# Four dense blocks instead of two in the head of a hybrid block, two of them before the norm is known

## The chip, the cores and the metric

The kernel runs on one core of a Trainium2 chip. The metric is the device time of one execution in microseconds; the median of three runs of the kernel before is 904.12 us. TensorE is PE in the profile, its weight loads PEld, VectorE is DVE, ScalarE is ACT, GpSimd is POOL, and SyncE, which issues most DMAs here, is SP.

## The reference, cut to what matters

One layer, 512 positions, width 1024. Only the first projection and what hangs on it matter here:

```
h    = rmsnorm(x) * g
P    = h @ w_in            # columns: attention q,k,v | RWKV r,k,v, decay, iclr, gate lora | branch gates
A    = stick_breaking_attention(q, k, v)              # 8 heads of 64
xs   = token_shift(P_rwkv, mu)                        # p + (previous p - p) * mu
w    = decay_base + tanh(w_lo) @ decay_up;  iclr = sigmoid(iclr_base + a_lo @ iclr_up)
y    = rwkv7_recurrence(r, decay, k, v, -kk, kk*iclr) # 8 heads of 64, chunks of 64 positions
x    = x + (sigmoid(gate_0) * (A @ W0) + sigmoid(gate_1) * (B @ W1)) @ w_out
x    = x + W_down(silu(c_g) * c_v),  [c_g, c_v] = causal conv3(rmsnorm(x) @ W_up)
```

The norm multiplies every position of h by one number, rs. A projection of x*g can therefore be multiplied by rs afterwards, before the token shift.

## The kernel before, in words

Activations lie with channels on partitions (8 tiles of 128) and the 512 positions on the free axis. Every fp32 operand of a dense product is split in a high part (fp32r) and the rest; a product of two is three matmuls: high by high, high by rest, rest by high. A **dense block** gives 128 columns of a projection: 8 tiles of the contraction by 3 is 24 matmuls of 128x128 by 128x512. Its weight comes by one DMA (load_w, line 102), ScalarE casts the high part (line 104), ScalarE writes minus the high part (line 117) and a DMA issued by GpSimd adds the raw weight to it (line 118). There are two raw and two high buffers and four of half a rest.

The **head** (lines 198 to 310) loads x (line 211), the weights of two blocks (line 206) and the small matrices; squares x on ScalarE, sums the squares over partitions by a matmul with a constant matrix (line 228), and makes rs with a logarithm and an exponential. Then, tile by tile, it makes xn = x g rs on VectorE (line 238), the high part on ScalarE (line 239) and the rest on VectorE or GpSimd (line 240), with six matmuls to each tile (lines 242 to 245): the lora block (pl0) and k of RWKV's first pair of heads (pk0). lora's result becomes wal and, by a tanh, wl1 and wl2; the two small matrices become lup (lines 269 to 271).

What follows is written by **a planner** (interleave). Six streams, one of dense blocks (dense_stream), one that runs the attention of four pairs of heads in turn (att_stream), and four of RWKV (rw_stream, one to a pair of heads), yield costs, delays (LAT) and events; the planner keeps a clock of its own and writes the instructions in the order that this clock gives. PE and SP execute in exactly that order; the other engines' order is chosen by the framework. A dense block is taken when no other stream is ready, or when a deficit has grown; RWKV's blocks are taken when the event prep of the pair before is near, then those of the attention, else a branch gate (evac_gate, line 785), of which 13 are written here.

A pair of RWKV goes through: two lora products (line 393), the norm of k (lines 153 and 154 by blk2), preparation (lines 438 to 468) with the same pair of lines at its end, four groups of transposes and products (lines 484 and 489), two stores and loads through DRAM, a **solve** of 31 steps on VectorE (lines 520 and 522), again a turn through DRAM to U1 and TT, the products that start from U1 (line 543), eight chunks one after another (lines 590 to 616), a norm, and the output gate (line 640). LAT says at what moment of the planner's clock something is due: k0=42000 holds all of pair 0 after lora back, and the second block of the stream as well; solve is about 50000.

When all streams have ended, what is left (three gates, w_branch, w_out, the feed-forward part) follows and is not touched by the change.

Of the kernel before, what the change touches and what calls it, by code (L numbers as in the profile page):

```python
# [8 lines left out]
F32 = mybir.dt.float32  # L9
F32R = mybir.dt.float32r  # L10
# [42 lines left out]
def hybrid_block(ctx: ExitStack, tc: tile.TileContext, xT, w_in, vecs, decay_up, iclr_up, out_gate_up,  # L53
# [24 lines left out]
    def f(ap):  # L78
        return ap.bitcast(F32)
# [17 lines left out]


    def load_w(src, nk):
# [4 lines left out]
        A.copy(hi[:, 0:nk], raw[:, 0:nk])  # L104
        w = (hi, [], raw)
        for _ in range(1 if nk <= 4 else 2):
            load_w2(w, nk)
        return w
# [87 lines left out]
    with tc.tile_pool(name="p0", bufs=1) as p0, \  # L196
# [10 lines left out]

        w0, w1 = wtiles(), wtiles()
        A.dma_start(vec, vecs[:, 0:NVEC1])
# [10 lines left out]
        V.tensor_copy(none_, tmpc)  # L220
        pl0, pn, pk0, rs = bank(psr, "pr"), bank(psr, "pr"), bank(), bank(psz, "pz")

        for k in range(0, KT, 2):
            sq = [p0.tile([P, T], F32, tag=f"sq{j}", name=f"sq{j}", bufs=2) for j in range(2)]
            for j in range(2):
                act(sq[j], xt[:, k + j], AF.Square)
            V.tensor_tensor(sq[0], sq[0], sq[1], op=ALU.add)
            PE.matmul(pn, f(none_), sq[0], start=(k == 0), stop=(k == KT - 2))
        act(rs, pn, AF.Ln, scale=-1.0 / D, bias=eps_n)
        act(rs, rs, AF.Exp, scale=-0.5)  # L230
        for w in (w0, w1):
            for h in range(2):
                A.copy(w[0][:, 4 * h : 4 * h + 4], w[2][:, 4 * h : 4 * h + 4])
                load_w2(w)

        for k in range(KT):
            xn = p0.tile([P, T], F32, tag="xn", name="xn", bufs=3)
            V.scalar_tensor_tensor(xn, xt[:, k], vcol("ag", k), rs, op0=ALU.mult, op1=ALU.mult)
            A.copy(hhi[:, k], xn)
            (V if k % 2 else G).tensor_tensor(hlo[:, k], xn, f(hhi[:, k]), op=ALU.subtract)  # L240
            for ps, w in (pl0, w0), (pk0, w1):
                PE.matmul(ps, w[0][:, k], hhi[:, k], start=(k == 0), stop=False)
                PE.matmul(ps, w[1][k // 4][:, k % 4], hhi[:, k], start=False, stop=False)
            for ps, w in (pl0, w0), (pk0, w1):
                PE.matmul(ps, w[0][:, k], hlo[:, k], start=False, stop=(k == KT - 1))
        state["dma"] = True
# [7 lines left out]
        V.tensor_scalar(qg8, vcol("qg"), 0.125, None, op0=ALU.mult)  # L254
        wfirst = load_w(w_in[:, RW0 : RW0 + P], KT)
        wal = p0.tile([P, T], F32, name="wal")
        shift_evac(wal, pl0, 12)
# [8 lines left out]
        for j in range(2):  # L266
            hr, ho = slice(64 * j, 64 * j + 64), slice(64 - 64 * j, 128 - 64 * j)
            lt = p0.tile([P, BW], F32R, tag="lt", name="lt")
            A.copy(lt, lraw[j])
            V.tensor_tensor(lup[j][ho], lraw[j][ho], f(lt[ho]), op=ALU.subtract)  # L270
            A.copy(lup[j][hr], lraw[j][hr])

# [74 lines left out]

    def evac_rw(p, which, ps):
        RD[p][which] = rwp.tile([P, T], F32, tag="x" + which, name="x" + which)
        shift_evac(RD[p][which], ps, 4 * "rkv".index(which) + p)  # L350
# [448 lines left out]
    def dense_stream():  # L799
        rwq, atq = [], []  # L800
        for p in range(4):
            for i, w in (1, "k"), (0, "r"), (2, "v"):
                if (p, w) != (0, "k"):
                    rwq.append((RW0 + i * BW + p * P, evac_rw, (p, w), w + str(p), (f"prep{p - 1}",)))
# [16 lines left out]

        evac_rw(0, "k", pk0)
        yield ("set", "k0", LAT["k0"])
        yield ("set", "bank-1", LAT["k0"])
        i, cur = 0, pick()
        nxt = wfirst
        while cur:
# [14 lines left out]
            else:  # L842
# [13 lines left out]
    FULL, SHORT = 0.65, 450  # L856
    LAT = dict(evac=5520, ahead=11059, k0=42000, gl0=1, gl1=2, att0=(1332, 762, 1125, 1575),
               att1=(810, 810, 810, 688), gn=(659, 3062, 2114, 3270), hop=(1073, 1254, 767, 762),
               lup=(8543, 2168, 5055, 862), pl=(671, 2115, 609, 2223), prep=(9000, 9000, 9000, 9000),
               pu=(1860, 2060, 1022, 1951), qk=(1409, 1644, 4330, 575), rw0=(792, 1679, 2305, 1342),  # L860
               solve=(46500, 49755, 50000, 50000), sq=(2447, 1872, 3786, 557), sq_a=(1958, 1741, 1565, 328),
# [206 lines left out]
```

## Time and profile before

| | |
|---|---|
| median of 3 runs | 904.12 us (903.95 to 909.15) |
| profiled execution | 908.44 us, of it 906.6 us span |
| PE busy | 864.9 us, 95% of the span, 4722 matmuls |
| PEld, DVE, ACT, POOL busy | 74%, 60%, 56%, 14% |
| chain that ended last | PE 80%, ACT 6%, DVE 5%, DMA 5%, issue 2% |

Busy time is a union of spans, and a matmul's span is longer than its distance to the next, so a PE that is shown as full need not be at its fastest. The distance from one matmul's start to the next one's is the better measure, and the moments at which the stages begin are better still.

### The profile page before, as it was taken

To read this page: it belongs to the slowest core of one execution; us is meant where nothing else is said; L and a number is where in the kernel's file an instruction comes from. 1 tells how busy PE (TensorE), PEld (TensorE's weight loads), DVE (VectorE), ACT (ScalarE), POOL (GpSimd) and SP (SyncE) were. 2 spreads that over 40 slices of the span, in tenths; PEclk is the share of its full clock that TensorE was granted. 3 is DMA by queue.
4 is the path that set the end of the run, shared out by engine and by line. 5 is a ranking of instruction groups with operands and counts; after the bars stand their busy time and mean duration, and the time that the engine had idled before them with its cause. 6 is when DMAs were issued, how large, how long until landed. Compare 5 with 4: busy or idle time off the path is not lost.

```text
span 906.6 us, 12925 instructions
## 1 busy us (share of the span) xinstructions
PE 864.9 (95%) x4722; PEld 668.4 (74%) x4722; DVE 544.6 (60%) x1104; ACT 508.0 (56%) x900; POOL 129.9 (14%) x200
## 2 busy tenths in 40 slices
PE   4988988999999999899999999999999999999998
PEld 2666756676767677667888888888888888888886
DVE  5466796685785484246565556777777777522222
ACT  6787877866875784688654445444444444311120
POOL 2323333224322332223000000000000000000000
PEclk8999999998999999999999999999999999999999
DMA  8276556556548445852654543333333333243431
GB/s 230 53 147 132 112 128 116 126 121 126 120 84 184 106 94 111 165 127 73 228 190 135 149 122 92 98 93 93 94 99 106 97 94 94 87 128 99 124 102 41
DMA packets 175135, 106.94 MB, mean 118 GB/s; under 512 B 29568, under 2 KB 156672, under 8 KB 175072
## 3 DMA queue, kind: packets, MB, share of 16 engines
q1 hardware_dynamic: 161392, 81.61, 32.1%
q0 software_dynamic: 10656, 19.40, 12.7%
q10 hardware_dynamic: 3024, 5.11, 1.6%
q8 instruction: 37, 0.61, 0.3%
q14 instruction: 26, 0.21, 0.1%
HBM read 78.31 MB, written 8.39 MB: 96 GB/s over the span
## 4 chain that ended last, share of the span: by engine, by line
PE 80%; ACT 6%; DVE 5%; DMA 5%; issue 2%; SPq 1%; POOL 1%; POOLq 0%; ACTq 0%
PE pf L130 17%; PE pf L131 17%; PE pf L132 17%; PE pd L847 15%; DMA wraw<-in_w_in 2%; DMA wlo<-wraw 1%; DVE tm L520 1%; SPq L529 1%; ACT whi L104 1%; PE pz L730 1%; PE pr L603 1%; PE pr L489 1%; PE pr L590 1%; ACT wlo L117 1%; ACT t L69 1%
## 5 line engine op out<-in xcount | busy, mean ns | idle before, releaser
L104 ACT CAST whi<-wraw 128x1024 fp32r<-128x1024 f32 (+1 forms) x132 | 130.0, 985 | 192.6 <-PE pf L131 143.6
L120 DVE TENSOR_TENSOR wlo<-wraw,whi 128x512 fp32r<-128x512 f32 (+1 forms) x178 | 114.5, 680 | 81.6 <-ACT whi L104 75.7
L130 PE MATMUL pf<-h2h,whi 128*128 128x512 f32 x352 | 137.3, 390 | 0.0
L131 PE MATMUL pf<-h2l,whi 128*128 128x512 f32 x352 | 136.9, 389 | 0.0
L132 PE MATMUL pf<-h2h,wlo 128*128 128x512 f32 x352 | 136.9, 389 | 0.0
L847 PE MATMUL pd<-hhi,whi 128*128 128x512 f32 x296 | 122.8, 415 | 6.5 <-ACT gs L785 2.8
L847 PE MATMUL pd<-hlo,whi 128*128 128x512 f32 x296 | 121.8, 411 | 0.0
L118 POOL DMA_DIRECT2D wlo<-wraw x74 | 65.1, 912 | 191.6 <-ACT wlo L117 111.8
L847 PE MATMUL pd<-hhi,wlo 128*128 128x512 f32 x296 | 86.0, 409 | 2.8 <-DMA wlo<-wraw 2.7
L131 PEld LDWEIGHTS pf<-h2l,whi 128*128 128x128 f32 x352 | 66.1, 188 | 13.9 <-issue 0.2
L132 PEld LDWEIGHTS pf<-h2h,wlo 128*128 128x128 f32 x352 | 66.1, 188 | 13.8
L130 PEld LDWEIGHTS pf<-h2h,whi 128*128 128x128 f32 x352 | 66.1, 188 | 13.8 <-issue 0.2
L847 PEld LDWEIGHTS pd<-hhi,whi 128*128 128x128 f32 x296 | 56.8, 192 | 20.5 <-ACT gs L785 3.3
L132 PE MATMUL pf<-dh,wlo 128*128 128x512 f32 x176 | 69.3, 394 | 0.0
L130 PE MATMUL pf<-dh,whi 128*128 128x512 f32 x176 | 69.3, 394 | 0.0
L131 PE MATMUL pf<-dl,whi 128*128 128x512 f32 x176 | 69.3, 394 | 0.0
L847 PEld LDWEIGHTS pd<-hhi,wlo 128*128 128x128 f32 x296 | 53.6, 190 | 17.4 <-DMA wlo<-wraw 5.9
L847 PEld LDWEIGHTS pd<-hlo,whi 128*128 128x128 f32 x296 | 56.8, 192 | 11.7 <-issue 0.5
L1007 DVE TENSOR_TENSOR u<-pf,rs 128x512 f32<-128x512 f32 x44 | 30.3, 688 | 38.7 <-PE pf L132 38.6
L124 ACT CAST dh<-cv 128x512 fp32r<-128x512 f32 x22 | 13.7, 621 | 62.0 <-DVE cv L1016 62.0
L117 ACT ACTIVATE wlo<-whi 128x512 fp32r<-128x512 f32 x74 | 45.5, 630 | 1.9 <-ACT QA L598 0.7
L130 PEld LDWEIGHTS pf<-dh,whi 128*128 128x128 f32 x176 | 32.9, 187 | 8.3
(303 smaller groups left out, 1609.6 us busy)
## 6 DMA issues: line engine op xcount, KB each, us to landing
wraw<-in_w_up SPq DMA_DIRECT2D x44, 512.0 KB, 3.7
wraw<-in_w_in SPq DMA_DIRECT2D x42, 512.0 KB, 3.9
wlo<-wraw POOLq DMA_DIRECT2D x74, 256.0 KB, 3.9
wraw<-in_w_down SPq DMA_DIRECT2D x16, 512.0 KB, 4.0
wraw<-in_w_branch SPq DMA_DIRECT2D x16, 256.0 KB, 2.9
wraw<-in_w_out SPq DMA_DIRECT2D x8, 512.0 KB, 4.0
gd<-gs ACTq DMA_DIRECT2D x13, 256.0 KB, 3.3
g<-gd SPq DMA_DIRECT2D x13, 256.0 KB, 2.9
```

Source lines behind the costliest of these rows:

```text
L69: ins = A.activation(o, i, func, **kw)
L104: A.copy(hi[:, 0:nk], raw[:, 0:nk])
L117: A.mul(lo[:, 0:n], f(hi[:, k0 : k0 + n]), -1.0)
L118: G.dma_start(lo[:, 0:n], raw[:, k0 : k0 + n], accum_op=ALU.add)
L120: V.tensor_tensor(lo[:, 0:n], raw[:, k0 : k0 + n], f(hi[:, k0 : k0 + n]), op=ALU.subtract)
L124: A.copy(hi, src)
L130: PE.matmul(ps, hi, ah, start=first, stop=False)
L131: PE.matmul(ps, hi, al, start=False, stop=False)
L132: PE.matmul(ps, lo, ah, start=False, stop=last)
L489: PE.matmul(pp[h][:, j * P : (j + 1) * P], BK[hr, ch].rearrange("p s t -> p (s t)"), ARV[hr, ch, 0 : 2 + h : 1 + h], start=True, stop=True)
L847: PE.matmul(ps, w_, a, start=(n == 0), stop=(n == len(todo) - 1))
L1007: V.tensor_tensor(u, ps, rs2, op=ALU.mult)
```

## The change

In the head, four blocks are computed. x and the weights are loaded in turns, in the order x0, half of w0, x1, half of w0, x2 and x3, half of w1, x4 and x5, half of w1, x6 and x7, w2, w3. As each tile of x lands, x g is split in high and rest and multiplied by lora's weight (w0) and, three tiles behind, by k's (w1); the rest-by-high matmuls of both come after. Then rs is made, and the same buffers are filled again with the normalised x, tile by tile, for r (w2) and v (w3) of pair 0. lora's result and k's are multiplied by rs afterwards (ul, and u in evac_rw), from a copy rss. The stream loses the blocks r0 and v0 and starts with q of the attention's first pair. k0, r0 and v0 are due 4000 after the stream's start (before: k0 at 42000), and rw0 goes from 792 to 2500. Some instructions of ScalarE are tied behind the last high part of the normalised x: the table load for tanh, the casts for lup, the high part of the first weight of the stream.

```
-        for k0, k1 in ((0, 1), (1, 2), (2, 4), (4, 6), (6, 7), (7, 8)):
-            nc.sync.dma_start(xt[:, k0:k1], xv[:, k0:k1])
-        wdma(w0, LR0, 0, 8)
-        wdma(w1, RW0 + BW, 0, 8)
+        nc.sync.dma_start(xt[:, 0:1], xv[:, 0:1])
+        wdma(w0, LR0, 0, 4)
...
+        wdma(w2, RW0, 0, 8)
+        wdma(w3, RW0 + 2 * BW, 0, 8)
...
+        def first(w, ps, k, part):
+            PE.matmul(ps, w[0][:, k], h_acts[k][part], start=(k + part == 0), stop=False)
+        def second(w, ps, k):
+            lo = w[1][k // 4][:, k % 4] if isinstance(w[1], list) else w[1][:, k]
+            PE.matmul(ps, lo, hhi[:, k], start=False, stop=(k == KT - 1))
+        LAG = 3
+        for k in range(KT):
+            if k % 4 == 0:
+                A.copy(w0[0][:, k : k + 4], w0[2][:, k : k + 4])
+            act(hhi[:, k], xt[:, k], AF.Identity, scale=vcol("ag", k))
+            V.scalar_tensor_tensor(hlo[:, k], xt[:, k], vcol("ag", k), f(hhi[:, k]), op0=ALU.mult, op1=ALU.subtract)
+            for part in range(2):
+                first(w0, pl0, k, part)
+            sq[k] = p0.tile([P, T], F32, name=f"sq{k}")
+            sql = act(sq[k], xt[:, k], AF.Square)
+            if k % 4:
+                V.tensor_tensor(sq[k & 4], sq[k & 4], sq[k], op=ALU.add)
+            if k % 4 == 3:
+                A.copy(w1[0][:, k - 3 : k + 1], w1[2][:, k - 3 : k + 1])
+            if k >= LAG:
+                for part in range(2):
+                    first(w1, pk0, k - LAG, part)
+            if k % 4 == 3:
+                PE.matmul(pn, f(none_), sq[k & 4], start=(k == 3), stop=(k == 7))
...
+        first_parts(w2, sql)
+        second_parts(w2, sql)
         act(rs, pn, AF.Ln, scale=-1.0 / D, bias=eps_n)
         act(rs, rs, AF.Exp, scale=-0.5)
...
-            A.copy(hhi[:, k], xn)
+            state["last"] = A.copy(hhi[:, k], xn)
             (V if k % 2 else G).tensor_tensor(hlo[:, k], xn, f(hhi[:, k]), op=ALU.subtract)
+            if k == 1:
+                first_parts(w3, state["last"])
+            if k == 3:
+                second_parts(w3, state["last"])
+            for part in range(2):
+                first(w2, pr0, k, part)
+            if k >= 2:
+                for part in range(2):
+                    first(w3, pv0, k - 2, part)
+            if k >= LAG:
+                second(w2, pr0, k - LAG)
...
+        after(A.copy(rss, rs), state["last"])
...
+        V.tensor_tensor(ul, pl0, rss, op=ALU.mult)
+        shift_evac(wal, ul, 12)
         load_set(SET_SG, (AF.Sigmoid, AF.Tanh))
+        after(state["load"], state["last"])
...
-                if (p, w) != (0, "k"):
+                if p > 0:
...
-        evac_rw(0, "k", pk0)
-        yield ("set", "k0", LAT["k0"])
-        yield ("set", "bank-1", LAT["k0"])
+        evac_rw(0, "k", pk0, by=rss)
+        evac_rw(0, "r", pr0)
+        evac_rw(0, "v", pv0)
+        for w in "krv":
+            yield ("set", w + "0", LAT["k0"])
+        yield ("set", "bank-1", LAT["evac"])
```

first_parts casts the high part of a weight in two halves on ScalarE; second_parts writes minus the high part on ScalarE and adds the raw weight by a DMA of GpSimd, as load_w2 does.

## Rows read from the trace of the kernel before

**Rows 1.** Stretches of the span: busy time and instructions of each engine, PEclk, DMA share, GB/s.

```profile
5.00:19.00 14.00, 7.42 (x8) 2.13 (x8) 7.28 (x14) 8.77 (x15) 0.00 (x0) 0.96 0.84 231
33.00:61.00 28.00, 24.58 (x95) 16.97 (x96) 11.09 (x16) 26.29 (x44) 10.46 (x15) 1.00 0.63 122
86.00:130.00 44.00, 40.61 (x191) 29.99 (x190) 36.91 (x98) 38.65 (x85) 18.36 (x26) 1.00 0.54 119
150.00:300.00 150.00, 145.60 (x1208) 107.12 (x1209) 102.34 (x286) 107.87 (x225) 42.13 (x67) 0.97 0.60 127
550.00:600.00 50.00, 50.00 (x222) 41.42 (x221) 37.39 (x56) 22.82 (x29) 0.00 (x0) 1.00 0.32 95
```

**Rows 2.** Timeline of the head: start, length, engine, line, operation, tiles.

```profile
3.62 1.32 ACT L69 ACTIVATE sq<-xt 128x512 f32<-128x512 f32 x2 [1.53 <-DMA xt<-in_xT]
...
11.57 0.63 ACT L69 ACTIVATE sq<-xt 128x512 f32<-128x512 f32 x1 [0.54 <-PE pr L228]
...
17.07 1.28 ACT L63 ACT_TABLE_LOAD   x1
...
18.36 0.62 ACT L239 CAST hhi<-xn 128x512 fp32r<-128x512 f32 x1
...
19.04 0.80 PE L242 MATMUL pr<-hhi,whi 128*128 128x512 f32 x1 [4.23 <-ACT hhi L239]
...
27.40 0.62 ACT L239 CAST hhi<-xn 128x512 fp32r<-128x512 f32 x1 [0.88 <-DVE xn L238]
...
32.23 0.39 PE L245 MATMUL pr<-hlo,whi 128*128 128x512 f32 x1
...
32.46 0.39 PE L245 MATMUL pd<-hlo,whi 128*128 128x512 f32 x1
...
32.66 1.04 ACT L104 CAST whi<-wraw 128x1024 fp32r<-128x1024 f32 x1 [4.63 <-PE pr L245]
...
33.75 0.50 PE L847 MATMUL pd<-hhi,whi 128*128 128x512 f32 x1 [0.91 <-ACT whi L104]
```

**Rows 3.** Stretches of 1 us in the head, columns as in rows 1.

```profile
18.00:19.00 1.00, 0.00 (x0) 0.00 (x0) 1.00 (x3) 0.99 (x3) 0.00 (x0) 0.50 0.00 0
...
25.00:26.00 1.00, 1.00 (x6) 0.83 (x5) 0.87 (x2) 0.93 (x3) 0.71 (x1) 1.00 0.00 0
```

**Rows 4.** ACT's groups, 33 to 87 us: count | busy us, mean ns | idle before.

```profile
L117 ACT ACTIVATE wlo<-whi 128x512 fp32r<-128x512 f32 x14 | 8.2, 619 | 0.0
L104 ACT CAST whi<-wraw 128x1024 fp32r<-128x1024 f32 x7 | 7.3, 1043 | 9.5 <-DMA wraw<-in_w_in 4.9 <-PE pr L245 4.6
```

**Rows 5.** Last products ahead of the solve, pairs 0 to 3: ns min/median/max, first and last start.

```profile
L489 PE MATMUL pr<-ARV,BK x32: 272/272/524, 71.2 to 85.7; 64*128 64x128 f32 x32
...
L489 PE MATMUL pr<-ARV,BK x32: 272/272/325, 138.6 to 155.4; 64*128 64x128 f32 x32
...
L489 PE MATMUL pr<-ARV,BK x32: 272/272/362, 206.1 to 217.2; 64*128 64x128 f32 x32
...
L489 PE MATMUL pr<-ARV,BK x32: 272/272/325, 292.1 to 306.0; 64*128 64x128 f32 x32
```

**Rows 6.** First products behind the solve, pairs 0 to 3, columns as in rows 5.

```profile
L543 PE MATMUL pr<-U,QA x32: 184/191/212, 150.0 to 150.5; 32*32 32x32 f32 x32
...
L543 PE MATMUL pr<-U,QA x32: 184/236/258, 219.0 to 220.5; 32*32 32x32 f32 x32
...
L543 PE MATMUL pr<-U,QA x32: 191/191/212, 286.7 to 287.2; 32*32 32x32 f32 x32
...
L543 PE MATMUL pr<-U,QA x32: 191/191/212, 375.1 to 375.6; 32*32 32x32 f32 x32
```

**Rows 7.** What PE waited for, 30 to 432 us: us in total, times, longest.

```profile
PE pr L543 <- DMA U<-st: 4.1, 3, 2.5
```

**Rows 8.** End of the streams: the last gates' copies and pair 3's output gate.

```profile
L785 ACT COPY gs<-pd x4: 587/588/623, 395.1 to 433.1; 128x512 f32<-128x512 f32 x4
...
L640 PE MATMUL pr<-gl,ogu x1: 399/399/399, 422.5 to 422.5; 96*128 96x512 f32 x1
```

More of the change, by code (lines that the diff above doesn't have):

```diff
@@ L96, in vcol, with after @@
         return vec[:, o : o + w] if o < NVEC1 else state["vec2"][:, o - NVEC1 : o - NVEC1 + w]
+    def after(ins, other):
+        tc.add_manual_dep(ins.ins, other.ins.name, _ORDER, reason="order")
     def load_w(src, nk):
@@ L103, in load_w @@
         hi = wpool.tile([P, KT, P], F32R, tag="whi", name="whi")
-        A.copy(hi[:, 0:nk], raw[:, 0:nk])
+        after(A.copy(hi[:, 0:nk], raw[:, 0:nk]), state["last"])
         w = (hi, [], raw)
@@ L220, in hybrid_block @@
         V.tensor_copy(none_, tmpc)
[L221 to L228, printed above, removed]
+        pl0, pn, pk0, pr0 = bank(psr, "pr"), bank(psr, "pr"), bank(), bank()
@@ new lines, in hybrid_block, with first_parts, second_parts @@
+        for w in (w0, w1):
+            load_w2(w)
+            load_w2(w)
+        for k in range(KT - LAG, KT):
+            for part in range(2):
+                first(w1, pk0, k, part)
+        for k in range(KT):
+            second(w0, pl0, k)
+            second(w1, pk0, k)
+        def first_parts(w, other):
+            for k in (0, 4):
+                after(A.copy(w[0][:, k : k + 4], w[2][:, k : k + 4]), other)
+        def second_parts(w, other):
+            for k in (0, 4):
+                after(A.mul(w[1][:, k : k + 4], f(w[0][:, k : k + 4]), -1.0), other)
+                G.dma_start(w[1][:, k : k + 4], w[2][:, k : k + 4], accum_op=ALU.add)
@@ L229, in hybrid_block @@
+        first_parts(w2, sql)
+        second_parts(w2, sql)
         act(rs, pn, AF.Ln, scale=-1.0 / D, bias=eps_n)
         act(rs, rs, AF.Exp, scale=-0.5)
[L231 to L234, printed above, removed]
+        rss = keep.tile([P, T], F32, tag="rs", name="rss")
         for k in range(KT):
@@ L268, in hybrid_block @@
             lt = p0.tile([P, BW], F32R, tag="lt", name="lt")
-            A.copy(lt, lraw[j])
+            after(A.copy(lt, lraw[j]), state["last"])
             V.tensor_tensor(lup[j][ho], lraw[j][ho], f(lt[ho]), op=ALU.subtract)
-            A.copy(lup[j][hr], lraw[j][hr])
+            after(A.copy(lup[j][hr], lraw[j][hr]), state["last"])
         ident = cpool.tile([P, P], F32, name="ident")
@@ L346, in hybrid_block, with evac_rw @@
     AD = [dict() for _ in range(4)]
-    def evac_rw(p, which, ps):
+    def evac_rw(p, which, ps, by=None):
+        if by is not None:
+            u = rwp.tile([P, T], F32, tag="u", name="u")
+            V.tensor_tensor(u, ps, by, op=ALU.mult)
+            ps = u
         RD[p][which] = rwp.tile([P, T], F32, tag="x" + which, name="x" + which)
```

33 lines of the change are left out of this document (24 added, 9 removed).

## The prediction

> **What bounds the kernel now.** I read the stretches first. Behind the streams PE is full and no other engine is near it (550 to 600 us in [rows 1]): nothing there is touched, so the question is only at what moment the streams end. They end at 433.1 us, with the last gate's copy [rows 8]. In the head PE is busy for 7.42 of 14 us while it waits for x and for rs, and ACT for 8.77 [rows 1]. From 33 to 61 us the picture turns: ACT is busy for 26.29 of 28 us, PE for 24.58 by spans that flatter it. From 86 to 130 us ACT is at 38.65 and DVE at 36.91 of 44. From 150 to 300 us no engine but PE is above three quarters, and PE's instructions are in an order written ahead, so small waits add up in it [rows 1].
>
> Then I marked the stages of the four RWKV pairs by two lines: the last product ahead of the solve (S: 85.7, 155.4, 217.2, 306.0) [rows 5] and the first one behind it (B: 150.0, 219.0, 286.7, 375.1) [rows 6]. From S to B a pair takes 64.3, 63.6, 69.5, 69.1 us, and PE waited in three of four cases for U1 itself, 4.1 us in all [rows 7]. So the solve and its two turns through DRAM are nearly as late as PE's order: neither alone sets the end.
>
> **The change, part by part.**
>
> *PE in the head.* Between matmuls 0.23 us pass (32.23 to 32.46, [rows 2]), so a block is 24 x 0.227 = 5.45 us. Before, two blocks end at 32.85, the stream starts at 33.75 [rows 2], and r0 and v0 cost it 10.9 us. After: the last of x landed for the square at 11.57 [rows 2]; now 1 MB of weights goes in turns with it, at the head's 231 GB/s [rows 1] at most 4.5 us; bounds 11.6 and 16, taken 13.7, as three of the four halves lie ahead of where x would otherwise be at the end. On ACT each tile now has a high part beside the square, 16 x 0.62 and four half casts, 12.4 us by full lengths, from the first landing at 3.6 [rows 2]: 16, so ACT and the last landing agree on about 16.3 for the last square. From the last square's start to the first normalised high part 6.8 us passed (11.57 to 18.36), 1.28 of it the table load that is now tied behind [rows 2]: 5.5 us. w2's four casts can slip in between at 0.62 each, 0 to 2.5. So the first normalised tile is cast at about 21.9 + 0.6 (bounds 20.5 and 24); the eight took 9.0 us (18.36 to 27.40, [rows 2]) and take as long again, since VectorE's and GpSimd's work on a tile is unchanged: 31.2. Behind the last tile about 20 matmuls are left, 4.5 us: PE ends the head at **35.8** (33.5 to 39). It is two blocks ahead of before at 32.85 + 0.9 + 10.9 = 44.7: a credit of 8.9 us.
>
> *ACT.* Two weights of the stream move into the head, 2 x (1.04 + 2 x 0.62) = 4.6 us [rows 4]. But the table load (1.28), four casts for lup (0.62 each) and the copy rss (0.6), of which the first five lay in ACT's idle time in the head, are now behind the last tile [rows 2]: 4.4 us. ACT's stage begins at 31.2 instead of 32.66. While ACT is full, which is so at least to 61 us, 1.5 us is all that can be cashed of the credit. The extra multiplications by rs are two of VectorE, 0.7 us each, which has 17 us idle from 33 to 61 [rows 1]; on the way of tanh and lup the first one is exposed, with rss and the table load about 3 us, and lup's product (third of the stream's groups) is where PE meets them: 0 to 4 us, inside S0 below.
>
> *The order that is planned.* Following the planner's rule with the new numbers (for the order alone): ahead of S of pair 0 stand q, k, v of attention, a gate, the two gate-lora blocks, another gate, and five of the eight attention jobs of pair 0. Before, it is r0, v0, q, k, v and most of a gate, and no job. Between S and B stand 7, 6, 6, 7 blocks, as before. Between B of pair 0 and S of pair 1: the solve's loads are now planned just behind the last group. Between B of pair 1 and S of pair 2: two more blocks and the four groups, where before S came first. Behind B of pair 3: two blocks instead of five, and no attention job where before there were all eight.
>
> *Queues.* On SP w2, w3 and the half-weights go ahead of the small matrices; nobody needs these before 31 us. On POOL two DMA adds of w2 and two of w3 stand among the four splits; w3's are wanted last of all. These cost nothing as long as a pair of adds ends in the 8 us that they have; if not, the head's end moves with them, inside its bound.
>
> **The sum**, against the profiled execution (908.44 us, 4.3 above the median; the difference is carried over to the median):
> - S of pair 0, before 85.7. At before's pace from a stream start of 35.8: 52 us, 1.4 blocks more (7.6) and five jobs at about a microsecond of PE (5): 100.4. Lower bound: the 3.4 us of PE idle of 33 to 61 and as many again are gone, 93.5. Upper bound: ACT sets it; all eight jobs lie in 86 to 130 with 38.65 us of ACT [rows 1], so five add at most 24: 85.7 - 1.5 + 24 = 108. Taken 100: **+14.3**. It is a loss that buys work done ahead.
> - S to B, four times: the same cover, and VectorE has half of pair 0's attention behind it in the first solve. Bounds -12 and 0; taken **-4**.
> - B0 to S1: 5.4 us become -1: **-6.4**.
> - B1 to S2: -1.8 become +18 (four groups 11.1 us with what lies between them [rows 5], one more block 5.45, a little): **+19.8**.
> - B2 to S3: 19.3 less a group and half a block: **-5.5**.
> - B3 to the end: 58.0 us (375.1 to 433.1); three blocks fewer, 16.4, and eight jobs fewer, some 8, but pair 3's chain alone is then what runs; taken 36 (bounds 33 and 47): **-22**.
>
> Together -3.8 us: 904.6 by the profiled execution, **900.3** on the median. The 8.9 us of credit is mostly spent on waiting for ACT and on a last pair with nothing beside it.
>
> **The rivals.**
> - *The credit is kept.* If PE rather than ACT sets S of pair 0 (93.5, so 6.5 less), and the solves come 8 us shorter in all because VectorE and ACT meet less work at once, 14 us more are gained, with half of it about 893 and with all of it 886; 890 as its centre. For it: no engine but PE is over three quarters from 150 us on [rows 1]. Against: ACT's 26.29 of 28.
> - *Slower: the last pair's chain.* From B of pair 3 to its output gate 46.9 us passed (375.1 to 422.0, from the four matmuls that end at 422.5 [rows 8]). If the eight chunks take that long by their own latency, whether or not blocks lie between them, the tail is 47 instead of 36: +11, so 911; with S of pair 0 at 104 it is 915. It decides from a tail of 40 us on. For it: each chunk waits for the one before. Against: five blocks and eight jobs of PE lie in that stretch.
> - *The first pass doesn't bring its end forward* (the change doesn't do what it says): x lands behind the weights, or PE's clock stays low. After its idle time PE had a granted clock of 0.50 from 18 us on, which is the 1.2 GHz level, and was back at 1.00 by 25 us, after about 5 us of matmuls [rows 3]. At 0.45 us instead of 0.227 the 22 matmuls between the sums and the normalised tiles cost 4.9 us more, and part of that is hidden under ACT's eight casts: head's end 39.3, time 900 to 904, say 903. The Trainium skill says (TensorE: Matmul & The Clock Gate, HAM oscillation — how this bites in real kernels) that bursts of matmuls with waits for DMA between them are set back to the low clock each time, which speaks against matmuls that follow the landing of x. The rows here show one such fall and no series of them; by that rule the head would end at 39.3 and this rival holds, otherwise 35.8.
>
> **How the numbers follow.** Chances: forecast 0.42, credit kept 0.30, last pair's chain 0.18, no earlier end 0.10. A measurement of this kernel tells about 1% from no change, 9 us: faster means below 895.1, slower above 913.2. Of the credit's 0.30 about 0.26 lies below 895, and of the forecast's 0.42 about 0.08: faster 0.34. Of the chain's 0.18 half lies over 913, and of the forecast (S at its upper bound with nothing given back) 0.07: slower 0.16. The rest, 0.50, is no change. The range goes from the credit's far end, 886, to the chain's 912.
>
> **What would show it.** PE's last head matmul at 33.5 to 39 us; normalised casts from 22 us; PE's clock in the first pass; S of pair 0 at 94 to 108 us with ACT full ahead of it; S to B of 60 to 69 us four times; S of pair 2 about 18 us behind B of pair 1; a tail of 33 to 40 us behind B of pair 3, with PE idle in it; everything behind the streams as long as before, 473 us. The prediction is wrong if S of pair 0 comes before 90 us, if the solves become clearly shorter than 60 us, or if PE has a long wait that is not in this list.

## The result: 1.4% slower, and the profile after

The changed kernel takes 917.96 us (median of 4 runs, 915.99 to 920.82) against 904.04 for the kernel before (903.61 to 909.15): a ratio of 1.0143, interval 1.0097 to 1.0189. Forecast were 900.3 us and a range up to 912. The profiled execution took 915.99 us, span 914.3. That is 7.5 us more than the profiled execution of before, 6 us less than the medians differ by: the profile of before is one of its longer runs, that of after the shortest of its four (and of the runs below, 2 and 3 lie further off in the execution that was profiled, 925.37 us against a median of 918.84 and 937.63 against 920.78, so the columns of run 3 are left empty). The rows below answer to 7.5 us.

One sentence of the description ahead of the prediction is to be corrected. TensorE takes exactly the written order only in the head block. In the streams the planner's order is what is written, but the framework may still move one of TensorE's instructions past another: both lora products (L469) stand ahead of all of q's matmuls in the machine, though the planner writes q first.

The head first, as a timeline of the kernel after (start, length, engine, line, operation; in brackets the idle time and what ended it). It answers to [rows 2].

```profile
31.15 0.62 ACT L294 CAST hhi<-xn 128x512 fp32r<-128x512 f32 x1 [2.99 <-DVE xn L293]
...
36.25 1.07 PE L245 MATMUL pr<-hhi,w3l 128*128 128x512 f32 x4
39.83 0.50 PE L469 MATMUL pr<-wl,lup 128*128 128x512 f32 x1 [2.51 <-ACT wl L336]
...
42.38 0.68 DVE L342 TENSOR_TENSOR lup<-lraw,lt 64x512 fp32r<-64x512 f32 x1 [2.45 <-ACT lt L341]
42.99 0.68 DVE L423 TENSOR_TENSOR u<-pd,rss 128x512 f32<-128x512 f32 x1
...
43.21 0.77 PE L469 MATMUL pr<-wl,lup 128*128 128x512 f32 x1 [2.45 <-DVE lup L342]
...
44.63 0.80 PE L927 MATMUL pd<-hhi,whi 128*128 128x512 f32 x1
...
52.01 0.39 PE L927 MATMUL pd<-hhi,whi 128*128 128x512 f32 x1
```

And the kernel before, from the end of its second block in the streams (the value block) to the start of its fourth:

```profile
46.97 2.47 PE L847 MATMUL pd<-hhi,wlo 128*128 128x512 f32 x8 [1.11 <-DMA wlo<-wraw]
...
49.51 0.46 PE L847 MATMUL pd<-hhi,whi 128*128 128x512 f32 x1
...
58.26 0.39 PE L847 MATMUL pd<-hhi,whi 128*128 128x512 f32 x1
```

The last normalised tile is cast at 31.15 and the head's last matmul ends at 37.3. Then part of the gain is lost again: both lora products wait, and q's first matmul needs the bank from which the first pair's key is scaled (L423); that stands on VectorE behind the second lora matrix. Dense work of the streams starts at 44.63. The kernel before has its receptance and value blocks done and starts q at 49.51, not at 44.7 as the prediction reckoned: from 33.75 the two blocks take 15.8 us, with both lora products and the wait of 1.11 us among them, where 10.9 were put down. So the kernel after is 4.9 us ahead when it starts q, and 6.2 us when it has done q (52.01 against 58.26).

The first pair's and the other pairs' last products ahead of the solve, then the first behind it (ns min/median/max, first and last start). They answer to [rows 5] and [rows 6].

```profile
L565 PE MATMUL pr<-ARV,BK x32: 271/273/581, 88.1 to 109.9; 64*128 64x128 f32 x32
...
L565 PE MATMUL pr<-ARV,BK x32: 271/272/525, 155.3 to 169.9; 64*128 64x128 f32 x32
...
L565 PE MATMUL pr<-ARV,BK x32: 271/272/525, 248.7 to 265.8; 64*128 64x128 f32 x32
...
L565 PE MATMUL pr<-ARV,BK x32: 271/272/524, 326.5 to 344.4; 64*128 64x128 f32 x32
...
L619 PE MATMUL pr<-U,QA x32: 190/191/212, 173.1 to 176.1; 32*32 32x32 f32 x32
...
L619 PE MATMUL pr<-U,QA x32: 227/236/256, 242.2 to 244.2; 32*32 32x32 f32 x32
...
L619 PE MATMUL pr<-U,QA x32: 228/236/257, 333.5 to 334.5; 32*32 32x32 f32 x32
...
L619 PE MATMUL pr<-U,QA x32: 190/191/213, 412.3 to 412.8; 32*32 32x32 f32 x32
```

S of the first pair is 24.2 us later, the first product of the last solve 37.2 later, and the tail behind that is short. The end of the streams, which answers to [rows 8]:

```profile
L716 PE MATMUL pr<-gl,ogu x1: 389/389/389, 439.9 to 439.9; 96*128 96x512 f32 x1
...
L861 ACT COPY gs<-pd x5: 566/585/587, 400.6 to 427.8; 128x512 f32<-128x512 f32 x5
```

And TensorE's longest wait from 30 to 441 us, which answers to [rows 7] (us in total, times, longest):

```profile
PE pr L619 <- DMA U<-st: 10.9, 2, 5.5
```

Now the last gate (427.8) comes ahead of the last pair's output gate (439.9): the chain ends the streams, not the blocks beside it. What follows the streams takes 473.8 us, before 473.7.

Then the stretches of the kernel after (columns as in [rows 1]; PEclk is the granted clock).

```profile
15.00:37.00 22.00, 20.53 (x86) 15.34 (x84) 14.32 (x19) 16.33 (x28) 10.63 (x11) 1.00 0.59 121
70.00:100.00 30.00, 27.60 (x100) 18.43 (x99) 20.53 (x37) 24.42 (x53) 7.79 (x10) 0.72 0.43 97
...
236.00:242.00 6.00, 0.80 (x4) 0.34 (x2) 0.00 (x0) 0.00 (x0) 2.47 (x7) 0.80 0.72 101
242.00:250.00 8.00, 7.85 (x86) 5.93 (x86) 3.44 (x6) 3.99 (x7) 0.00 (x0) 0.51 0.68 157
```

And of the kernel before, the stretch to compare with the second:

```profile
70.00:100.00 30.00, 27.86 (x159) 20.50 (x158) 17.22 (x35) 24.73 (x56) 9.98 (x17) 0.94 0.61 134
```

Here lies a trap in reading: from 70 to 100 us TensorE is busy for the same time in both, 27.60 and 27.86 us, but after it does 100 matmuls and before 159. At a granted clock of 0.72 the same busy time is less work. Over the whole stretch from the first matmul to the streams' end, added up over TensorE's rows, after is idle for 31.4 us (before 31.9) and spends 40.8 us of its busy time at 0.50, the 1.2 GHz level (before 22.2). Half of the difference is 9.3 us. Less 0.5 us of idle time and 1.4 us of work, counted at full clock, it gives the 7.4 us by which this stretch is longer. This is an identity and not yet a cause, but it says where to look: at the stretches at 0.50, which are 41.7 to 48.5 (behind the idle head), 82.6 to 99.7, 157.7 to 164.6, 239.7 to 249.9 and 331.8 to 338.6. The two last follow waits of 5.4 and 5.5 us at the first product behind a solve, as the rows of 236 to 250 show for one.

### The profile page after: what moved, and what is told of

Its sections match the earlier page's. It is cut to its first block, busy times and chain, and to the rows that moved or that the text cites. A ratio compares the mean times of both kernels' runs of the same rounds, so it can differ in the third digit from the quotient of the medians.

```text
span 914.3 us, 12944 instructions
## 1 busy us (share of the span) xinstructions
PE 873.0 (95%) x4718; PEld 677.6 (74%) x4718; DVE 552.4 (60%) x1116; ACT 513.0 (56%) x911; POOL 130.7 (14%) x200
## 4 chain that ended last, share of the span: by engine, by line
PE 76%; DVE 9%; ACT 7%; DMA 4%; issue 2%; SPq 1%; POOL 1%; ACTq 0%; POOLq 0%; DVEq 0%
PE pf L136 17%; PE pf L135 17%; PE pf L134 17%; PE pd L927 11%; DMA wraw<-in_w_in 2%; DMA su<-U 1%; ACT t L69 1%; PE pr L565 1%; PE pr L679 1%; PE pz L806 1%; DVE U L598 1%; PE pr L666 1%; DVE tm L596 1%; PE pr L560 1%; ACT wlo L121 1%
## 5 line engine op out<-in xcount | busy, mean ns | idle before, releaser
L108 ACT CAST whi<-wraw 128x1024 fp32r<-128x1024 f32 (+2 forms) x130 | 128.0, 985 | 183.7 <-PE pf L135 144.3
L927 PE MATMUL pd<-hhi,whi 128*128 128x512 f32 x280 | 115.7, 413 | 0.0
L927 PE MATMUL pd<-hlo,whi 128*128 128x512 f32 x280 | 115.1, 411 | 0.0
L122 POOL DMA_DIRECT2D wlo<-wraw x70 | 62.0, 935 | 157.0 <-ACT wlo L121 87.3
L927 PE MATMUL pd<-hhi,wlo 128*128 128x512 f32 x280 | 82.4, 413 | 1.3 <-DMA wlo<-wraw 1.1
L136 PEld LDWEIGHTS pf<-h2h,wlo 128*128 128x128 f32 x352 | 66.1, 188 | 13.6
L927 PEld LDWEIGHTS pd<-hhi,whi 128*128 128x128 f32 x280 | 54.4, 194 | 11.9 <-issue 1.1
L927 PEld LDWEIGHTS pd<-hlo,whi 128*128 128x128 f32 x280 | 54.3, 194 | 11.1 <-issue 0.2
L927 PEld LDWEIGHTS pd<-hhi,wlo 128*128 128x128 f32 x280 | 51.6, 193 | 14.4 <-DMA wlo<-wraw 3.6
L128 ACT CAST dh<-cv 128x512 fp32r<-128x512 f32 x22 | 13.7, 621 | 62.0 <-DVE cv L1096 62.0
L121 ACT ACTIVATE wlo<-whi 128x512 fp32r<-128x512 f32 x70 | 42.8, 628 | 2.4 <-PE pd L927 1.1
L135 PEld LDWEIGHTS pf<-dl,whi 128*128 128x128 f32 x176 | 33.0, 187 | 8.2
```

Of the source, the lines that this page charges most:

```text
L108: after(A.copy(hi[:, 0:nk], raw[:, 0:nk]), state["last"])
L121: A.mul(lo[:, 0:n], f(hi[:, k0 : k0 + n]), -1.0)
L122: G.dma_start(lo[:, 0:n], raw[:, k0 : k0 + n], accum_op=ALU.add)
L128: A.copy(hi, src)
L135: PE.matmul(ps, hi, al, start=False, stop=False)
L136: PE.matmul(ps, lo, ah, start=False, stop=last)
```

## The experiments

All stand against the kernel before on the same chip. S0 is the first pair's last product ahead of its solve, "end" the first matmul behind the streams, idle is TensorE's idle time and low the time for which its clock is 0.50, busy or not (so 47.8 and 23.9 where 40.8 and 22.2 above count the busy part), from its first matmul to that end. S0, end, idle and low are in us, from the one profiled execution of each run.

| | what is altered | ratio (interval) | S0 | end | idle | low |
|---|---|---|---|---|---|---|
| before | | 1 | 85.7 | 432.9 | 31.9 | 23.9 |
| after | | 1.0143 (1.0097 to 1.0189) | 109.9 | 440.5 | 31.4 | 47.8 |
| 1 | new head, old due times | 1.015 (1.0135 to 1.0166) | 97.0 | 441.7 | 28.7 | 37.5 |
| 2 | old head, new due times | 1.016 (1.0117 to 1.0204) | 106.3 | 449.9 | 31.2 | 61.4 |
| 3 | after, key scaled in the head | 1.016 (1.0131 to 1.0188) | | | | |
| 4 | 3 with old due times | 1.0142 (1.0103 to 1.0181) | 96.8 | 440.2 | 27.0 | 34.1 |
| 5 | after, lora dues 1000 | 1.01 (1.0064 to 1.0135) | 89.1 | 438.8 | 30.9 | 37.5 |
| 6 | 5 and 3 | 1.011 (1.0078 to 1.0142) | 89.2 | 439.1 | 29.6 | 34.1 |
| 7 | after, gate lora later | 1.0193 (1.0155 to 1.0231) | 104.7 | 442.0 | 36.5 | 28.1 |
| 8 | 6 and 7 | 0.9998 (0.9977 to 1.0019) | 89.8 | 430.1 | 23.9 | 27.3 |
| 9 | after, solve dues longer | 1.019 (1.0167 to 1.0214) | 110.9 | 446.2 | 31.9 | 62.2 |
| 10 | 8, solve dues longer | 1.0065 (1.0035 to 1.0096) | 89.3 | 432.3 | 29.9 | 17.1 |
| 11 | before, 40 matmuls left out | 1.0011 (0.9986 to 1.0035) | 89.9 | 435.1 | 33.4 | 37.5 |
| 12 | half the head | 0.9986 (0.9966 to 1.0005) | 85.8 | 427.6 | 29.3 | 20.5 |
| 13 | 8, lora's chain ahead | **0.9932** (0.991 to 0.9953) | 85.7 | 422.3 | 26.9 | 13.7 |
| 14 | 12, weight cast free | 0.9972 (0.9955 to 0.9989) | 84.6 | 425.4 | 23.8 | 20.5 |
| 15 | 14, lora's chain ahead | 1.0018 (1.0001 to 1.0035) | 87.6 | 431.7 | 28.2 | 30.7 |
| 16 | 3, lora's chain ahead | 1.023 (1.0184 to 1.0277) | 108.8 | 443.9 | 35.3 | 48.0 |
| 17 | 5 and 7 | **0.9953** (0.9929 to 0.9977) | 90.9 | 424.2 | 23.2 | 13.7 |

**1 and 2. The halves of the change.** Each half alone: the head with the old due times, the old head with the new ones.

```diff
-    LAT = dict(... k0=4000, ... rw0=(2500, ...
+    LAT = dict(... k0=42000, ... rw0=(792, ...
-        yield ("set", "bank-1", LAT["evac"])
+        yield ("set", "bank-1", LAT["k0"])
```

> The changed kernel with the planner's old due times (k0=42000 for k0, r0, v0 and the second block, rw0=792): the head of four blocks alone. If the planning is what costs (theory P: gate lora and five attention jobs stand ahead of pair 0's transposes, which end at 109.9 us instead of 85.7), the transposes of pair 0 end at 80 to 92 us and the time is 890 to 904. If the late start of q (theory Q: its bank is free only at 43.7 us, 7 us after the head, and the clock falls) is what costs, the time stays at 912 to 918. If the head itself costs (theory H), it stays above 910 and the transposes stay late.

> The kernel before with k0=4000, rw0=2500 and the second block's bank due at 5520: the planning alone, with two blocks in the head. P: slower than before, 909 to 920, with pair 0's last product ahead of the solve later than 95 us. Q and H: no change, 902 to 906, since its first block has a free bank and its head is the old one.

918.79 and 918.84 us. Each half costs what the whole does, so costs don't add. The second is as theory P has it, the first isn't: with the old due times S0 comes at 97.0 and nothing is won. Theory Q's range for the first, 912 to 918, is missed by 0.8 us.

**3 and 4. The late start of q.** The key is scaled right behind the lora's sum, so that its bank is free; 3 with the new due times, 4 with the old ones.

```diff
         V.tensor_tensor(ul, pl0, rss, op=ALU.mult)
+        uk = keep.tile([P, T], F32, tag="uk", name="uk")
+        V.tensor_tensor(uk, pk0, rss, op=ALU.mult)
...
-        evac_rw(0, "k", pk0, by=rss)
+        evac_rw(0, "k", uk)
```

> The changed kernel with one instruction moved: k0's multiplication by rs stands right behind lora's, in a tile of its own, so that q's bank is free about 9 us earlier. Q: PE goes on at 37 to 38 us, the clock stays at its upper level there, streams end 9 to 11 us earlier, 905 to 909. P: the 7 us are waited for again ahead of pair 0's transposes, which move by less than 3 us, and the time is 913 to 918. H: 913 to 918.

> Both: the early multiplication and the old due times. If P and Q are two costs that add up, 882 to 895, faster than before; if only P holds, as with the old due times alone; if only Q holds, as with the early multiplication alone.

920.78 and 916.66 us; the first is above every range given, and the second isn't the sum of two gains (882 to 895). In both dense work starts at 37.6 instead of 44.6, and nothing comes of it. The late start isn't the cause by itself.

**5 to 8. The planner's numbers.** With the chain planned at once, the first pair's plan holds two dues of 8543 ns behind its decay products (`yield (427, LAT["lup"][p])`). In the kernel before they ran out while the planner waited for the key's due of 42000.

```diff
-               lup=(8543, 2168, 5055, 862), ...
+               lup=(1000, 2168, 5055, 862), ...
```

and for 7 and 8

```diff
-    LAT = dict(... gl0=1, gl1=2, ...
+    LAT = dict(... gl0=3, gl1=4, ...
```

> The changed kernel with one number altered: the due time that the planner puts behind each of the first pair's two decay products, 8543 to 1000. Seen so far: from the first pair's last product ahead of its solve (S0) to the end of the streams it takes 347.2 us in the kernel before, 344.7, 343.6 and 343.4 in the three variants with one half of the change or with the earlier scaling, 330.6 in the changed kernel; what they lose is S0 itself (85.7 before; 109.9, 97.0, 106.3 and 96.8). Theory D (due times): planned at once, the first pair waits out two dues of 8.5 us that lay beside the head in the kernel before; with them at 1 us the planner's own time for S0 falls by 16.3 us (45.9 to 29.6 from the streams' start), so S0 comes to 94 to 100 and the whole to 901 to 910, at or just under the kernel before. Theory N (the order of the streams fits the kernel before, any other order loses): 914 to 922 whatever S0 does. Theory C (contention: the vector and scalar engines, full of attention and gate work, set S0, not the plan): S0 stays over 105 and the time at 915 to 922.

> The same due time of 1000, and the first pair's key scaled by the norm inside the head, so that q's block no longer waits for its bank (it started 7 us sooner with that alone, with no gain in the whole). Theory D: S0 follows the streams' start, 7 us sooner than with the due time alone: S0 88 to 94, whole 895 to 904. Theory N: 914 to 922. Theory C: S0 over 103, whole 914 to 920.

> The changed kernel with the gate lora's two blocks at places 3 and 4 of the queue of gate blocks in place of 1 and 2; the planner puts them at 47 and 94 us after the streams' start in place of 24 and 31, S0 stays where it is (46.6 for 45.9). Theory D: S0 105 to 111, whole 913 to 920, as the changed kernel. Theory G (the gate lora's chain of eight operations on the scalar and vector engines, ahead of the first pair's, holds S0): S0 97 to 101, whole 903 to 910. Theory N: 914 to 922.

> All three: due time 1000, the key scaled in the head, the gate lora at places 3 and 4 (planned at 124 and 131 us). Theory D: as with the first two, S0 88 to 94, whole 895 to 904. Theory G: 4 to 8 us better than that, 888 to 900. Theory N: 914 to 922.

914.9, 916.28, 923.72 and 904.67 us. The first product group of 5 and of 6:

```profile
L565 PE MATMUL pr<-ARV,BK x32: 272/272/373, 73.6 to 89.1; 64*128 64x128 f32 x32
```

```profile
L567 PE MATMUL pr<-ARV,BK x32: 272/272/373, 73.7 to 89.2; 64*128 64x128 f32 x32
```

S0 falls by 20.8 us, more than theory D said, and it is the same to 0.1 us whether the streams' dense work starts at 44.0 or at 38.4. So the plan sets S0, not TensorE's pace from the streams' start, and theory C is out. But the whole gains 3 us at most (1.01 for 1.0143, with intervals that overlap), inside theory N's range of 914 to 922 and not D's: D has the fall of S0 right and the end wrong. The later gate lora alone gains nothing (923.72 us is above all three ranges, and G is out as it was put: S0 104.7); with the shorter dues and the key scaled early it brings 11.6 us (run 8 against 6). N falls with 8, which is another order altogether and level with the kernel before.

**9 and 10. The waits behind the solve.** The solve's due times raised, in the changed kernel and in 8.

```diff
-               solve=(46500, 49755, 50000, 50000), ...
+               solve=(46500, 56000, 57000, 50000), ...     # 9
+               solve=(51000, 55000, 50000, 50000), ...     # 10
```

> The changed kernel with two numbers altered: the planner's due time for the solve of pairs 1 and 2, 49755 and 50000 to 56000 and 57000. In the changed kernel TensorE, which takes its work in the planned order, stands 5.35 us ahead of the first product behind pair 1's solve and 5.52 us ahead of pair 2's, and the granted clock is 0.50 in 239.7:249.9 and 331.8:338.6, right behind these waits. So far the time from the first matmul to the end of the streams is idle time plus 383 to 391 us of work at the full clock plus half of the busy time at the low clock: before 31.9 idle and 22.2 busy low, changed kernel 31.4 and 40.8. Theory W (such waits, and the low clock behind them, are what the change pays): both go, at most 10.9 + 8.5 = 19 us, half of it if other work can't fill all: 899 to 910. Theory N (any order but that of the kernel before costs 10 to 15 us): 914 to 922. Theory L (the pairs' chain is the bound, and a later product only makes it longer): 920 to 930.

> The variant with the shorter lora dues, the key scaled in the head and the later gate lora (904.67), with the solve's due of pairs 0 and 1 at 51000 and 55000 in place of 46500 and 49755. There TensorE stands 3.2 us ahead of pair 0's first product behind the solve and 3.9 us ahead of pair 1's, with the clock at 0.50 in 151.2:164.9 and 236.5:243.3. Theory W: up to 7.2 + 10.2 us go, half at least: 887 to 897, faster than both kernels. Theory N: 903 to 918. Theory L: 908 to 915.

923.56 and 910.71 us: theory W misses both. In 9 the waits for U go, but the products come 9 and 12 us later, TensorE waits elsewhere and the low clock grows from 47.8 to 62.2 us. In 10 the low clock does shrink, from 27.3 to 17.1, and another wait takes the place, 5.0 us for the gate lora at the first pair's output gate:

```profile
PE pr L718 <- ACT gl0h L69: 5.0, 1, 5.0
```

So those waits can't be had for free. Theory L's ranges, 920 to 930 and 908 to 915, hold both.

**11. What is a dense block worth in the streams?** Of two gate blocks 20 of 24 matmuls each are left out of the kernel before.

```diff
-                    PE.matmul(ps, w_, a, start=(n == 0), stop=(n == len(todo) - 1))
+                    cut = name in ("g00", "g01")
+                    if not cut or n % 6 == 0:
+                        PE.matmul(ps, w_, a, start=(n == 0), stop=(n == (18 if cut else len(todo) - 1)))
```

> The kernel before, leaving out 20 of the 24 matmuls of each of two of the gate's dense blocks (so their values are not the gate's); weights, copies and the order stay. What is a dense block worth in the streams? The change moves two of them into the head. Theory B (TensorE's work bounds the streams: busy 374 of 399 us in them): 40 matmuls of about 0.23 us, 9 us: 893 to 898. Theory L (the four pairs' chain is the bound): 902 to 906.

906.96 us, 1 us over theory L's range: nothing is gained by some 9 us less work. The stretch around the first of the two blocks, in this kernel and then in the kernel before:

```profile
74.00:90.00 16.00, 13.77 (x64) 9.41 (x62) 6.60 (x12) 11.10 (x23) 3.79 (x6) 0.57 0.39 84
```

```profile
74.00:90.00 16.00, 13.86 (x87) 10.04 (x86) 10.10 (x19) 13.70 (x29) 5.27 (x9) 0.89 0.47 108
```

23 matmuls fewer are found in the stretch, the busy time is the same, and the clock is 0.57 instead of 0.89. Added up, idle time grows by 1.5 us and time at the low clock by 13.6. Over all executions the granted clock has a median of 0.9805 here (10 executions) and 0.986 in the kernel before (25). Theory B is out: a dense block at this place is filler, and without it the clock is lower and the time is the same. Whether the low clock sets the time there, or the pairs' chain does and the clock falls beside it, isn't shown: S0 comes 4.2 us later than before, and the first product behind its solve at the same 150.0 us.

**12, 14 and 15. Half the head.** The two blocks from x as it lands stay in; receptance and value go back into the streams, with the due times of before and the key scaled early.

```diff
-        w2, w3 = (tuple(...) for n in (2, 3))
...
-            for part in range(2):
-                first(w2, pr0, k, part)
...
-                if p > 0:
+                if (p, w) != (0, "k"):
```

14 also takes `state["last"]` off the cast in `load_w`; 15 puts the lora's chain (scaling, tanh, its table, casts) behind the fourth normalised tile.

> Half the head: the two blocks from x as it lands (scaled by the norm afterwards, the key inside the head), the first pair's receptance and value blocks left in the streams as in the kernel before, and its due times too. Theory B: the two blocks' work lies under x's arrival, the streams' first block can start with the last normalised tile at 29 to 33 in place of 33.8, and nothing else is moved: 898 to 905. Theory N: any shift of the order costs: 914 to 922. Theory H (the vector and scalar work of the first pass itself, 16 operations more on each, costs the head more than it gives): 906 to 913.

> Half the head (904.21; both blocks done at 24.6, then TensorE idle for 6.7 us until the receptance block's weight is cast behind the last normalised tile), with that cast no longer tied behind the last tile. TensorE then takes the receptance block tile by tile from 22 to 31. Theory F (dense work is filler; what it wins early comes back as idle time or low clock, as when 40 matmuls were left out): 902 to 906. Theory B (TensorE's work bounds the streams): 5 to 6 us of idle time go, 896 to 900.

> Half the head with both: the weight's cast free, and the lora's chain behind the fourth normalised tile. Theory C48: first decay product 33 to 36 in place of 37.8, S0 81 to 84 in place of 85.8, whole 897 to 901. Theory E or F: 902 to 906. Theory N: over 912.

904.21, 903.6 and 907.43 us. In 12 both blocks are done at 24.6 us, 8 earlier than before, and then TensorE is idle for 6.7 us, behind the tied cast:

```profile
24.18 0.39 PE L241 MATMUL pd<-hhi,wlo 128*128 128x512 f32 x1
31.27 0.79 PE L901 MATMUL pd<-hhi,whi 128*128 128x512 f32 x1 [6.70 <-ACT whi L108]
```

The first pass does no harm: 12 can't be told from the kernel before, while the same due times with all four blocks in the head (run 4) cost 1.4%. Filling the 6.7 us brings 0.6 us on the median, with intervals that overlap, as theory F has it. In 15 the first lora product starts at 35.3 instead of 40.3, and S0 comes later (87.6): C48 is out, though run 13 below meets its S0 and its time, and why 15 is slower than 14 stays open. The 907.43 us of 15 lie between the ranges of F and N. H and N are out with 12.

**13, 16 and 17. Which edit carries it.** The lora's chain ahead, in 8 and in 3; and the two planner edits on the changed kernel with nothing else.

```diff
             (V if k % 2 else G).tensor_tensor(hlo[:, k], xn, f(hhi[:, k]), op=ALU.subtract)
+            if k == 3:
+                lora()       # ul, uk, wal, tanh, wl2, wl1, lup: from behind the loop
```

> The variant with four blocks in the head, short lora dues, the key scaled in the head and the later gate lora (904.67; first decay product 40.5, S0 89.8), with the lora's chain (scaling, tanh and its table, casts) put in behind the fourth normalised tile in place of behind the eighth. Theory C48 (S0 is the first decay product plus 48 to 50 us, the end follows S0 at 0.8 to 1): product at 34 to 37, S0 83 to 86, whole 898 to 902. Theory E (the end is set by the last attention pair and the blocks it waits for, whatever S0 does, as when the dues were shortened): 902 to 908 with S0 83 to 86. Theory D0 (the last normalised tiles come 5 us later, and q's block and all dense work with them): 906 to 912.

> The changed kernel with the key scaled in the head and the lora's chain behind the fourth normalised tile, the planner's dues and the gate lora's places untouched (17000 ns of dues stand behind the first pair's decay products in the plan, the gate lora's blocks third and fourth). Theory D (the plan of the first pair holds it back): first decay product 32 to 33, S0 still 98 to 110, whole 912 to 921. Theory C48 (S0 follows the first decay product): S0 81 to 90, whole 898 to 906.

> The changed kernel with the two planner edits alone (dues 1000, gate lora's blocks at places 3 and 4), its head untouched: q's first block waits for its bank to 44 and the clock falls there, as in the changed kernel. Theory D: S0 88 to 91 and 903 to 909, the level of the kernel before, so that the plan alone undoes the loss. Theory Q (the idle 7 us behind the head count too once the plan is mended): 909 to 915, that is the level with the shorter dues alone or a little under it.

898.62, 924.71 and 901.42 us. In 13 S0 and the time are as C48 has them, but not the step between: the first lora product starts at 32.2, 53.5 us ahead of S0 and not 48 to 50. 16 against 17 is the clearest pair of the study. With the first lora product 8 us sooner and the planner's numbers untouched, S0 hardly moves and the time is 2.3% over the kernel before; with two planner numbers altered and the head untouched, idle start and all, it is 0.5% under it. First the product group of 16, then of 17:

```profile
L571 PE MATMUL pr<-ARV,BK x32: 272/272/579, 89.4 to 108.8; 64*128 64x128 f32 x32
```

```profile
L565 PE MATMUL pr<-ARV,BK x32: 272/272/373, 75.4 to 90.9; 64*128 64x128 f32 x32
```

Why do the dues need the gate lora's place as well? 5 and 17 have the same S0 within 2 us and differ by 13.5. First 5: a dense group from 100 to 170 us (busy us, mean ns, idle before), TensorE's longest wait in these 70 us, and the stretch right behind it:

```profile
L927 PE MATMUL pd<-hhi,whi 128*128 128x512 f32 x42 | 16.9, 402 | 2.2 <-ACT whi L108 2.2
```

```profile
PE pr L619 <- DMA U<-st: 4.1, 1, 4.1
```

```profile
149.00:163.00 14.00, 13.26 (x92) 9.48 (x93) 4.79 (x8) 7.92 (x14) 2.11 (x3) 0.52 0.58 125
```

Then the group and the stretch in 17, where no wait for U is in the list:

```profile
L927 PE MATMUL pd<-hhi,whi 128*128 128x512 f32 x54 | 21.7, 402 | 0.0
```

```profile
149.00:163.00 14.00, 14.00 (x154) 9.96 (x154) 9.10 (x16) 11.28 (x22) 6.02 (x8) 1.00 0.58 125
```

The first product behind the solve comes at about the same time, 149.7 and 149.0 us. In 5 the gate lora's narrow block stands at 118 us, there are fewer dense matmuls around the solve's end, TensorE waits 4.1 us and then does 92 matmuls at 0.52 where 17 does 154 at 1.00, though not of the same mix. In 17, with the gate lora at 213 us, no such wait is seen, and S of the second pair comes 6.2 us earlier (160.3 against 166.5).

That the later gate lora covers this wait isn't the whole answer, and run 8 speaks against it. Its gate lora stands at 219 us, and yet TensorE waits 3.2 us at the same product and then runs at 0.58:

```profile
149.00:163.00 14.00, 13.27 (x94) 9.14 (x95) 4.80 (x8) 7.92 (x14) 2.19 (x3) 0.58 0.56 123
```

Run 6, the same but for the gate lora's place, waits 3.6 us there and does 93 matmuls at 0.51. The two stand level up to S of the last pair (311.0 and 311.1), and the 9.0 us between their ends (439.1 and 430.1) lie behind it. First 6, then 8, from there to the end:

```profile
311.00:439.00 128.00, 121.75 (x970) 90.91 (x969) 64.65 (x175) 87.50 (x193) 38.04 (x58) 0.97 0.54 118
```

```profile
311.00:430.00 119.00, 116.62 (x972) 88.27 (x971) 64.68 (x174) 87.38 (x193) 38.61 (x58) 1.00 0.58 129
```

Nearly the same matmuls take 128 us with 6.3 us of idle time in 6, and 119 us with 2.4 in 8. Of the 6.3, 3.9 us are two waits of the attention's products for ScalarE (L775), which 8 doesn't have. Why the gate lora's place brings these about stays open.

17 came out 1.6 us under what theory D said, so Q, by which the idle time behind the head should count now, finds nothing.

## Why the prediction was wrong

**The head was right as far as it went.** Normalised casts were put from 21.9 to 31.2 (measured 21.07 to 31.15), PE's last head matmul at 35.8, bounds 33.5 to 39 (37.3). The rival "first pass doesn't bring its end forward" is out: the clock from 15 to 37 us is 1.00, where before it fell at 18 [rows 3]. The Trainium skill has the rule that was weighed there (TensorE: Matmul & The Clock Gate, HAM oscillation — how this bites in real kernels): bursts of matmuls between waits for DMA start again at the low clock. In the head this doesn't show. In the streams the trace agrees once: from 236 to 242 us there is a wait for U's DMA, and 242 to 250 run at 0.51.

**Of the credit about half was left when the streams began.** The step that gave "0 to 4 us, inside S0" to the lora's longer way left out who is queued behind it. VectorE's scaling of the key stands behind the second lora matrix, q's bank behind that, and dense work starts at 44.63, 8.8 us after the 35.8 that was put down. The other end of the credit was mis-sized too: the receptance and value blocks cost the kernel before 15.8 us (33.75 to 49.51) and not 10.9. So 4.9 us were left at q's start and 6.2 at its end, and S of pair 0 is 24.2 us late all the same. Runs 3, 4 and 6 start dense work 6 to 7 us sooner, and none gains, so this omission isn't what the time hangs on.

**The step that failed is the term for S of pair 0**, +14.3 with bounds to 108; measured +24.2 (109.9). It was priced as the old pace from a stream start, plus 1.4 blocks and five attention jobs. By this formula and the true start, 44.6 + 64.6, it comes out at 109.2, but that agreement is chance: runs 5 and 6 start 5.6 us apart and have the same S0. The order had been worked out rightly, with q, k, v, a gate and the gate lora ahead of S0, yet I took it as given, not as something set by two dues that lost their cover. Taking these to 1000 ns moves S0 by 20.8 us (run 5). ScalarE, by which the upper bound was set, is busy for 24.42 of the 30 us from 70 to 100, where before it was 24.73, so it isn't fuller there.

The other terms, forecast against measured, from the rows of S and B:

- S to B four times: −4 against +4.6. Pair 1 alone is 8.5 longer (72.2 for 63.7): there TensorE waits 5.4 us at the first product behind the solve. With the 5.5 us of pair 2 this is the long wait that the prediction named as a sign of being wrong.
- B0 to S1: −6.4 against −8.5. B1 to S2: +19.8 against +25.5. B2 to S3: −5.5 against −8.5.
- B3 to the end: −22 against −29.8 (28.2 for 58.0). The rival "last pair's chain" named the right end of the streams, but not the price: from the last solve's first product to the output gate it is 27.6 us, not 47, once no blocks and jobs lie between.

Together +7.5 instead of −3.8 on the profiles. So the signs were right but one, and the sizes of S0, S to B and B1 to S2 carry 24 us of error, of which 13 came back in the tail and the other two terms. Nor do the terms stand alone, as a sum of them needs: in run 5 S0 is mended, and the tail behind B3 grows from 28.2 to 56.6 us (382.2 to 438.8), so that the end moves by less than 2 us. S0 is the term that was mis-sized, but its 24 us aren't by themselves the loss.

**What the sum couldn't see** is that TensorE's time isn't a fixed price per instruction. I counted blocks at 0.227 us a matmul wherever they stood. Run 11 shows that two blocks fewer in the streams are worth nothing, and that the clock falls where the first of them was. Run 4 against run 12 comes nearest to the change itself: with the receptance and value blocks moved from the streams to the head, the due times and the early scaling alike, the time is 12.5 us longer (916.66 against 904.21). The low clock lasts for 34.1 us instead of 20.5, and half of the difference, 6.8 us, is the most that it can have cost. The planned order moves with the blocks, and what the rest is isn't shown. In the changed kernel the longest stretch at the low clock is 82.6 to 99.7 us. The narrow gate lora ends at 81.7, and up to 95.1 TensorE has attention products and the first pair's transposes and products, and no dense block.

**The rival "credit is kept"** (890) asked for S of pair 0 at 93.5 and solves 8 us shorter in all. As the change stands neither holds: 109.9, and 4.6 us longer. With the two planner numbers mended both do (run 17: 90.9, and S to B 10.7 us shorter in all), and the time is 901.42 us, not 890. The change and the two numbers together are worth 0.5% (run 17), with the key scaled early and the lora's chain ahead too 0.7% (run 13, 898.62 us, the fastest version found; the intervals of the two overlap). What the same two numbers do to the kernel before wasn't run, so how much of this is the change's own stays open. So does why the two planner edits act only together, and run 15.

## What to carry to other kernels

Due times and hand-set costs in a planner are part of the change: one that was harmless because it ran out under another wait becomes a price when that wait goes, so follow each of them before you sum. Work moved out of a stage that is bound by a chain may have been its cover; price the move at zero until the trace shows that something else fills the place. And read busy time beside the granted clock and the count of instructions, never alone.

## What the runs showed of the hardware

Leaving out matmuls can leave the time as it was: 64 instead of 87 matmuls in 16 us took 13.77 us instead of 13.86, at a granted clock of 0.57 instead of 0.89 (run 11 and the kernel before, 74 to 90 us). A wait of 4.1 us at one product was followed by 14 us at 0.52 (run 5, 149 to 163 us). By an estimate from that clock 14 x 0.48 = 6.7 us of full clock are missing there, more than the wait itself.
